# Four edits to the order of work in a four-layer trunk kernel: summing DMA, first squares, attention order, last weights

## The chip, the cores and the metric

The kernel runs on one core of one Trainium2 chip. The metric is the device time of one execution in microseconds (us). Each time is one run; the runs of the kernel before are shown below.

## The reference

The reference is a trunk of four residual layers on 512 tokens of width 1024, in float32, and a last RMS norm. The layers are pooling, short convolution, latent attention, pooling. Each normalises x, widens it with one input projection, forms a branch of width 2048 and a gate of the same width, and adds the output projection of branch times silu(gate):

```python
def pool_mixer(xn, w_in, w_grp, scale, w_out):
    u, z = split(xn @ w_in, 2)
    # per group g of 512 channels: trailing mean over 2/4/8/16 tokens, minus the token
    mixed = einsum('bsgc,gcd->bsgd', pooled, w_grp) * scale
    return (mixed * silu(z)) @ w_out

def conv_mixer(xn, w_in, conv_w, w_out):
    b, c, h, z = split(xn @ w_in, 4)
    return (b * causal_depthwise_conv(c * h, conv_w) * silu(z)) @ w_out

def mla_mixer(xn, cos, sin, w_in, q_norm, w_q_up, kv_norm, w_kv_up, w_out):
    q_lat, kv_lat, k_rope, z = split(xn @ w_in, ...)       # 384, 256, 64, 2048
    q = rms_norm(q_lat) @ w_q_up                           # 16 heads x (128 + 64 rotary)
    k_nope, v = rms_norm(kv_lat) @ w_kv_up                 # 16 heads x 128 each
    o = causal_block_attention(q_nope, rope(q_rope), k_nope, rope(k_rope), v)
    return (o * silu(z)) @ w_out
```

## The kernel before, in words

x is held transposed, as eight tiles of 128 channels by 512 tokens. Every operand of a matmul is split into a high and a low part of the reduced float32 form: ACT copies the tile into the high part, and DVE subtracts that from the tile for the low part. A product is then three matmuls (`mm3`, L258 to L260: high by high, low by high, high by low). So each block of weights needs a load, one copy on ACT and one subtraction on DVE ahead of TensorE.

The layers are written as two streams of jobs (class `Stream`). A job is a `CHUNK` (128 by 1024 weights, 24 matmuls of 512 columns) or a `PAIR`. Step j of a stream issues the loads of jobs j+1 and j+2, then runs job j, and at eight positions in it calls small steps: the splits of job j+1 and what the jobs before left over. A position over 7 falls into the next job (its number less 8). Raw weights lie in four buffers of 1024 columns ("wr") and two of 512 ("wq"), split ones in six.

A `PAIR` makes two output tiles by seven half-width products instead of eight (`seven`, L388 to L460). It needs r (1024 columns: "wr" in the profile), r4 (512: "wq") and s13 (1024: "s", in a "wr" buffer too), which is the same 512 columns loaded twice (L119, SP's queue) with r's source added to it by a summing DMA on GpSimd's queue (L120). Its splits have fixed places: ah (from r) at position 4, al and sh (from s13) at 5, sl and ch (from r4) at 6, cl and the sums into r and r4 (L399, L400) at 7, th at 10 and tl at 11 (L393 on ACT, L396 on DVE). A summing DMA waits until both halves have landed, and a load waits until the last reader of its buffer is done: r of a later pair takes the buffer of an earlier s13, whose last reader is L399; s13 takes that of an earlier r, whose last reader is tl.

Only TensorE, ACT and DVE follow the order written in a stream. GpSimd, SP and the whole attention loop are ordered by a scheduler that knows the dependences.

The pooling layers multiply u by R (the scale of the norm, L322, L580), sum it over a window on GpSimd (L617, one to four adds), subtract on DVE (L623 to L625) and split. The first layer starts on x while it loads (`first_two`, called as `pre`): it makes the high and low parts of each tile of x (L348, L349) and multiplies at once; R follows from the squares of x (L276, L282), their sum over channels on TensorE, and a broadcast (`close`, L295 to L322). "Forms" (L359 to L382) are four sums and differences of neighbouring tiles of x, which `seven` needs.

In attention, head h goes through `scores` (L1018 to L1030, softmax with it, normalised on GpSimd in L1032), `turn_p` (ten transposes, pj, L1045), and `mix` (values by turned scores, po, L1057 to L1060). `stage_a(h+1)` makes queries and keys of the next head (pq and pk, 15 matmuls) and splits them (qh, ql, kh, kl: L158, L161). For every fourth head sixteen copies of the rotary part are issued on SP (L993, "qrs").

The tail is the second pooling layer's output projection, with tokens on the partitions. `token_major` runs three quarters of it as jobs; the last quarter follows the stream, with four more loads (L1249) and eight splits of 512 columns (L158, L161, `split`).

Of the kernel before, what the change touches and what calls it, by code (L numbers as in the profile page):

```python
# [23 lines left out]
H = 16  # L24
# [40 lines left out]
def trunk_kernel(ctx: ExitStack, tc: tile.TileContext, a):  # L65
# [28 lines left out]
    def f(t):  # L94
        return t.bitcast(F32)
# [17 lines left out]
    def load_pair(src):  # L113

        r, r4, s13 = wt("wr", "wr", F32), wp.tile([P, S], F32, tag="wq", name=nm("wq"), bufs=2), wt("s13", "wr", F32)
        nc.sync.dma_start(r, src[:, :CH])
        nc.sync.dma_start(r4, src[:, CH + S :])
        for q in range(2):
            nc.sync.dma_start(s13[:, q * S : (q + 1) * S], src[:, CH : CH + S])  # L119
        nc.gpsimd.dma_start(s13, src[:, :CH], accum_op=ALU.add)  # L120
        return r, r4, s13

# [62 lines left out]
    class Stream:  # L185
# [3 lines left out]
        def __init__(self):  # L189
            self.jobs, self.at, self.later, self.raw, self.ready = [], 0, Steps(), {}, {}  # L190

# [3 lines left out]
        def load(self, j):  # L195
            if j < len(self.jobs) and j not in self.raw:
                kind, src, _ = self.jobs[j]
                self.raw[j] = kind[0](src) if kind else None

# [14 lines left out]
        def step(self):  # L214
            j = self.at
            self.at += 1
            self.load(j + 1)
            self.load(j + 2)
            now, self.later = self.later, Steps()
            now.put(self.prepare(j + 1), 2 if self.jobs[j][0] is PAIR and self.jobs[j + 1 :] and self.jobs[j + 1][0] is not PAIR else 0, first=True)  # L220
            self.jobs[j][2](self.ready.pop(j, None), now)
            now(7)
            left, self.later = self.later, Steps()
            self.later.put(now.at, -8)
            self.later.put(left.at)
# [7 lines left out]
    def load_chunk(src, width=CH):  # L233
        raw = wt("wr", "wr", F32, width)
        nc.sync.dma_start(raw, src)
        return raw

# [14 lines left out]
    def wchunk(src, width=CH, pool=False):  # L252
        w, steps = prepare_chunk(load_chunk(src, width), width, pool)
        Steps(steps)(2)
        return w
# [540 lines left out]
    def mla_layer(stream, xn, begin, cos_sin, nxt):  # L796
# [273 lines left out]
        for h in range(H):  # L1070
# [10 lines left out]
            scores(h)  # L1081
            extra(1)
            if h:
                mix(h - 1)
            extra(2)
            if h + 1 < H:
                stage_a(h + 1)
            extra(3)
# [31 lines left out]
    def first_two():  # L1120

        pre = [ps("pt") for _ in range(2)]
        for k in range(KD):
# [16 lines left out]
            for m in range(2):  # L1140
                wh, wl = w0[m, hf]
                if k == m == 0:
# [4 lines left out]
                    continue  # L1147
                mm3(pre[m], wh[:, c], wl[:, c], *xn0.xs[k], first=(k == 0), last=(k == KD - 1))

        for m in range(KD):  # L1150
            s1.later.put({m: [lambda m=m: xn0.st.add(xt[m])]})
        s1.later.put({10: [xn0.st.close]})
        for kk in range(KK):
            s1.later.put(xn0.forms(kk), 24 + 16 * kk)
        return pre

    pool_layer(s1, 0, xn0, half, at=(4, 6), pre=first_two)
    xn = nxt
# [24 lines left out]

    def token_major(stream, c, hf, ys, then):

        pos = []

        def run(wl, now, kp):
            if kp == 0:
                pos.extend(ps("po") for _ in range(NT))  # L1190
# [16 lines left out]
    tail = {}  # L1207

    def last_half(hf, ys):
        if hf == 0:  # L1210
            for c in range(2):
                token_major(s2, c, 0, ys, add_tok)
        else:
            token_major(s2, 0, 1, ys, finish)
            tail["ys"] = ys
# [29 lines left out]
    ys = tail["ys"]  # L1245
    wres = {}
    for kk in range(4):
        raw = wt("wr", "wr", F32)
        nc.sync.dma_start(raw, w[1, 4 + kk])  # L1249
        for e in range(2):  # L1250
            wres[2 * kk + e] = split(raw[:, e * S : (e + 1) * S], "w")
    for i in range(NT):
# [116 lines left out]
```

## Time and profile before

| what | us |
| --- | --- |
| median of 3 runs (lowest, highest) | 1501.44 (1498.5, 1502.46) |
| the profiled execution: its own time, its span | 1502.28, 1500.5 |
| TensorE busy in the span | 1451.2 |
| DVE, ACT, GpSimd busy | 1086.7, 686.9, 258.3 |

The profile is of one execution. Times in it count from the start of its span. A row of waits gives an engine, the line that waited, what released it, the us in total, the times and the longest. In a row of the timeline, the first number is the start and the second how long the group was busy; what stands in brackets is the idle time of the engine before it and what ended that. "PEclk" is the clock granted to TensorE as a share of full speed.

### The profile page before, as it was taken

How to read it: one execution, taken by the hardware profiler on the slowest of the kernel's cores; microseconds unless marked ns; L12 is line 12 of the kernel's file. 1: busy time of each engine (PE TensorE's matmuls, PEld its weight loads, DVE VectorE, ACT ScalarE, POOL GpSimd, SP SyncE). 2: the span in 40 equal slices, each digit the busy share in tenths (PEclk: the TensorE clock that was granted, in tenths of full speed). 3: DMA queues.
4: the chain of work that ended last, by engine and by line, in shares of the span. 5: the costliest groups of instructions: out<-in, count | busy, mean ns of one | idle time of the engine just before them, and what ended most of it. 6: DMA issues, size and time to landing. Idle time of an engine off the chain costs nothing. (4 is left out here: it accounts for less than half of the span.)

```text
span 1500.5 us, 22412 instructions
## 1 busy us (share of the span) xinstructions
PE 1451.2 (97%) x8560; PEld 1273.3 (85%) x8560; DVE 1086.7 (72%) x1771; ACT 686.9 (46%) x1174; POOL 258.3 (17%) x291
## 2 busy tenths in 40 slices
PE   9999999999999999999999999999999999999997
PEld 7788797888999889999879988788888798888886
DVE  5885556659988878998688976667755487655854
ACT  4352233445554425555355655555633355323333
POOL 2413106021001000000211001121201122311502
PEclk9999999999999999999999999999999999999999
DMA  6243354325676457666236642122122434343431
GB/s 229 70 121 105 102 137 99 127 89 120 179 185 162 139 125 191 168 181 194 86 97 169 159 148 74 55 66 84 43 84 85 113 106 115 132 108 117 113 113 57
DMA packets 65147, 181.71 MB, mean 121 GB/s; under 512 B 8080, under 2 KB 8080, under 8 KB 65040
## 3 DMA queue, kind: packets, MB, share of 16 engines
q1 hardware_dynamic: 56688, 151.44, 31.7%
q0 software_dynamic: 7488, 27.27, 10.9%
q8 instruction: 67, 1.10, 0.3%
q10 hardware_dynamic: 864, 1.57, 0.3%
q14 instruction: 40, 0.33, 0.1%
HBM read 173.70 MB, written 2.10 MB: 117 GB/s over the span
## 5 line engine op out<-in xcount | busy, mean ns | idle before, releaser
L248 DVE TENSOR_TENSOR wl<-wr,wh 128x1024 fp32r<-128x1024 f32 (+1 forms) x140 | 173.1, 1236 | 55.9 <-ACT wh L245 54.7
L245 ACT ACTIVATE wh<-wr 128x1024 fp32r<-128x1024 f32 (+1 forms) x140 | 144.4, 1034 | 147.7 <-PE o L259 47.7
L260 PE MATMUL o<-yh,wl 128*128 128x512 f32 x384 | 151.3, 394 | 1.9 <-DVE wl L248 1.9
L259 PE MATMUL o<-yl,wh 128*128 128x512 f32 x384 | 151.3, 394 | 0.2 <-DVE yl L667 0.2
L258 PE MATMUL o<-yh,wh 128*128 128x512 f32 x384 | 150.9, 393 | 0.1
L260 PE MATMUL pt<-xh,wl 128*128 128x512 f32 x367 | 145.3, 397 | 4.0 <-DVE wl L248 4.0
L258 PE MATMUL pt<-xh,wh 128*128 128x512 f32 x367 | 146.2, 398 | 2.7 <-ACT wh L245 2.5
L259 PE MATMUL pt<-xl,wh 128*128 128x512 f32 x367 | 145.2, 396 | 0.6 <-DVE xl L349 0.6
L396 DVE TENSOR_TENSOR sl<-s,sh 128x1024 fp32r<-128x1024 f32 x52 | 65.4, 1259 | 35.2 <-ACT sh L393 32.8
L440 ACT ACTIVATE kept<-bv 128x256 f32<-128x256 f32 x52 | 19.9, 383 | 152.6 <-PE bv L426 90.7
L260 PEld LDWEIGHTS o<-yh,wl 128*128 128x128 f32 x384 | 72.1, 188 | 19.2 <-DVE wl L248 2.8
L260 PEld LDWEIGHTS pt<-xh,wl 128*128 128x128 f32 x367 | 69.5, 189 | 21.6 <-DVE wl L248 5.3
L259 PEld LDWEIGHTS o<-yl,wh 128*128 128x128 f32 x384 | 72.1, 188 | 17.2 <-DVE yl L667 0.5
L258 PEld LDWEIGHTS o<-yh,wh 128*128 128x128 f32 x384 | 72.1, 188 | 17.0 <-ACT yh L664 0.5
L258 PEld LDWEIGHTS pt<-xh,wh 128*128 128x128 f32 x367 | 69.5, 189 | 19.9 <-ACT wh L245 3.8
L259 PEld LDWEIGHTS pt<-xl,wh 128*128 128x128 f32 x367 | 69.5, 189 | 16.5 <-DVE xl L349 1.0
L120 POOL DMA_DIRECT2D s<-in_conv_in x30 | 26.0, 865 | 329.6 <-DMA s<-in_conv_in 105.4
L617 POOL TENSOR_TENSOR s<-u 128x527 f32<-128x527 f32 x32 | 50.0, 1562 | 180.6 <-DVE u L580 146.5
L282 POOL TENSOR_TENSOR sq<-sq,sq 128x512 f32<-128x512 f32 x25 | 39.6, 1585 | 211.3 <-ACT sq L276 210.9
L396 DVE TENSOR_TENSOR al<-wr,ah 128x1024 fp32r<-128x1024 f32 x52 | 64.1, 1233 | 14.2 <-ACT ah L393 12.1
L617 POOL TENSOR_TENSOR s<-s 128x525 f32<-128x525 f32 (+2 forms) x48 | 69.8, 1454 | 14.4 <-PE pm L259 11.1
L393 ACT ACTIVATE sh<-s 128x1024 fp32r<-128x1024 f32 x52 | 54.9, 1055 | 35.1 <-DMA s<-in_conv_in 17.8
(308 smaller groups left out, 4575.2 us busy)
## 6 DMA issues: line engine op xcount, KB each, us to landing
wr<-in_conv_in SPq DMA_DIRECT2D x34, 512.0 KB, 5.6
wr<-in_pool_out SPq DMA_DIRECT2D x32, 512.0 KB, 3.3
wr<-in_pool_u SPq DMA_DIRECT2D x30, 512.0 KB, 3.9
s<-in_conv_in SPq DMA_DIRECT2D x60, 256.0 KB, 4.6
s<-in_conv_in POOLq DMA_DIRECT2D x30, 512.0 KB, 6.2
wr<-in_pool_z SPq DMA_DIRECT2D x18, 512.0 KB, 4.0
wr<-in_pool_grp SPq DMA_DIRECT2D x16, 512.0 KB, 3.3
wr<-in_conv_out SPq DMA_DIRECT2D x16, 512.0 KB, 3.5
```

Of the source, the lines that this page charges most:

```text
L120: nc.gpsimd.dma_start(s13, src[:, :CH], accum_op=ALU.add)
L245: nc.scalar.activation(h, raw, AF.Copy)
L248: (nc.gpsimd if pool else nc.vector).tensor_tensor(out=l, in0=raw, in1=f(h), op=ALU.subtract)
L258: nc.tensor.matmul(out, ah, bh, start=first, stop=False)
L259: nc.tensor.matmul(out, ah, bl, start=False, stop=False)
L260: nc.tensor.matmul(out, al, bh, start=False, stop=last)
L282: eng.tensor_tensor(out=self.sum, in0=self.sum, in1=sq, op=ALU.add)
L393: return lambda: nc.scalar.activation(h, t, AF.Copy)
L396: return lambda: nc.vector.tensor_tensor(out=l, in0=t, in1=f(h), op=ALU.subtract)
L440: nc.scalar.activation(dst, src, AF.Copy)
L617: nc.gpsimd.tensor_tensor(out=nx[:, lo:], in0=cur[:, lo:], in1=cur[:, lo - d : S + PAD - d], op=ALU.add)
```

## The change

1. `load_pair` issues the two halves of s13 first, then r and r4. The summing DMA is no longer issued with them: it is a small step at position 4 of the same job.
2. First layer: the squares of x stand between the tiles of `first_two` (those of tiles 0 to 5; the last two follow at position 0 of the next job). Their sum is closed at position 3 instead of 10, the rows of the statistic stand at 3 and 5 instead of 4 and 6, and the four forms stand at 48, 56, 64, 72 instead of 24, 40, 56, 72.
3. Attention: `stage_a(h + 1)` stands ahead of `mix(h - 1)`.
4. The loads and splits of the last quarter's weights become small steps of the last four jobs of the stream (`resident`): loads at positions 0 or 4, copies on ACT at 8 to 13, subtractions on DVE two positions later.

```diff
     def load_pair(src):
 
-        r, r4, s13 = wt("wr", "wr", F32), wp.tile([P, S], F32, tag="wq", name=nm("wq"), bufs=2), wt("s13", "wr", F32)
+        s13 = wt("s13", "wr", F32)
+        for q in range(2):
+            nc.sync.dma_start(s13[:, q * S : (q + 1) * S], src[:, CH : CH + S])
+        r, r4 = wt("wr", "wr", F32), wp.tile([P, S], F32, tag="wq", name=nm("wq"), bufs=2)
         nc.sync.dma_start(r, src[:, :CH])
         nc.sync.dma_start(r4, src[:, CH + S :])
-        for q in range(2):
-            nc.sync.dma_start(s13[:, q * S : (q + 1) * S], src[:, CH : CH + S])
-        nc.gpsimd.dma_start(s13, src[:, :CH], accum_op=ALU.add)
-        return r, r4, s13
+        return (r, r4, s13), {4: [lambda: nc.gpsimd.dma_start(s13, src[:, :CH], accum_op=ALU.add)]}
...
             now, self.later = self.later, Steps()
+            now.put(self.loads.at)
+            self.loads = Steps()
...
             scores(h)
             extra(1)
+            if h + 1 < H:
+                stage_a(h + 1)
+            extra(2)
             if h:
                 mix(h - 1)
-            extra(2)
-            if h + 1 < H:
-                stage_a(h + 1)
             extra(3)
...
-        for m in range(KD):
-            s1.later.put({m: [lambda m=m: xn0.st.add(xt[m])]})
-        s1.later.put({10: [xn0.st.close]})
+            if k >= 2:
+                xn0.st.add(xt[k - 2])
+
+        for m in range(KD - 2, KD):
+            s1.later.put({0: [lambda m=m: xn0.st.add(xt[m])]})
+        s1.later.put({3: [xn0.st.close]})
         for kk in range(KK):
-            s1.later.put(xn0.forms(kk), 24 + 16 * kk)
+            s1.later.put(xn0.forms(kk), 48 + 8 * kk)
         return pre
 
-    pool_layer(s1, 0, xn0, half, at=(4, 6), pre=first_two)
+    pool_layer(s1, 0, xn0, half, at=(3, 5), pre=first_two)
...
+    def resident(now, kp):
+
+        for kk, n, at in ((0, 0, 8), (1, 0, 12), (2, 1, 12), (3, 2, 10)):
+            if n == kp:
+                raw = wt("wr", "wr", F32)
+                wres.update({2 * kk + e: (ut("wh", F32R), ut("wl", F32R)) for e in range(2)})
+                now.put({4 if kp else 0: [lambda raw=raw, kk=kk: nc.sync.dma_start(raw, w[1, 4 + kk])]})
+                for e in range(2):
+                    (h, l), half = wres[2 * kk + e], raw[:, e * S : (e + 1) * S]
+                    now.put({at + e: [lambda h=h, half=half: nc.scalar.activation(h, half, AF.Copy)],
+                             at + 2 + e: [lambda h=h, l=l, half=half: nc.vector.tensor_tensor(out=l, in0=half, in1=f(h), op=ALU.subtract)]})
...
-            token_major(s2, 0, 1, ys, finish)
+            token_major(s2, 0, 1, ys, finish, resident)
...
-    wres = {}
-    for kk in range(4):
-        raw = wt("wr", "wr", F32)
-        nc.sync.dma_start(raw, w[1, 4 + kk])
-        for e in range(2):
-            wres[2 * kk + e] = split(raw[:, e * S : (e + 1) * S], "w")
```

SP's queue in the convolution layer, two pairs, before: L116 is r (wr), L119 the two halves of s13 (s), L117 is r4 (wq).

```order
L116 DMA wr_3497<-in_conv_in 128x1024
L119 DMA s_668_3499<-in_conv_in 128x512 x2
L117 DMA wq_3498<-in_conv_in 128x512
L116 DMA wr_3630<-in_conv_in 128x1024
L119 DMA s_687_3632<-in_conv_in 128x512 x2
L117 DMA wq_3631<-in_conv_in 128x512
```

The same place now (L117 the halves, L119 r, L120 r4):

```order
L117 DMA s_666_3497<-in_conv_in 128x512 x2
L119 DMA wr_3500<-in_conv_in 128x1024
L120 DMA wq_3501<-in_conv_in 128x512
L117 DMA s_685_3630<-in_conv_in 128x512 x2
L119 DMA wr_3633<-in_conv_in 128x1024
L120 DMA wq_3634<-in_conv_in 128x512
```

The halves of s13 have changed places with r. They wait for what r waited for (L399 of an earlier pair), and r waits for what they waited for (tl).

TensorE in a head of the attention loop, before: the end of the key product (pk) and the first transposes (pj); the twelve matmuls of the value mix (po) stand ahead of pq and pk there.

```order
L258 MATMUL pk_10851<-lnh_8439,wh_10360 128x512
L259 MATMUL pk_10851<-lnl_8440,wh_10360 128x512
L260 MATMUL pk_10851<-lnh_8439,wl_10361 128x512
L1045 MATMUL pj_10875<-con,p_10773 128x128
L1045 MATMUL pj_10875<-con,p_10774 128x128
```

The same place now, from the end of pk into the value mix; the other four of po and the transposes follow.

```order
L261 MATMUL pk_10837<-lnh_8439,wh_10346 128x512
L262 MATMUL pk_10837<-lnl_8440,wh_10346 128x512
L263 MATMUL pk_10837<-lnh_8439,wl_10347 128x512
L1060 MATMUL po_10848<-th_10695,vh_10133 128x512
L1061 MATMUL po_10848<-tl_10696,vh_10133 128x512
L1062 MATMUL po_10848<-th_10695,vl_10134 128x512
L1060 MATMUL po_10848<-th_10697,vh_10144 128x384
L1061 MATMUL po_10848<-tl_10698,vh_10144 128x384
L1062 MATMUL po_10848<-th_10697,vl_10145 128x384
L1060 MATMUL po_10848<-th_10699,vh_10155 128x256
L1061 MATMUL po_10848<-th_10699,vh_10155 128x256
```

The value mix has moved in between the key product and the transposes, after which the next scores read the split keys.

ACT at the end of the program, before: the last copies of the stream's chunks (wh, L245), the four squares of the finished rows (fsq), and then the copies of the last quarter's weights (wh, L158).

```order
L245 ACTIVATE wh_14657<-wr_14618 128x1024
L245 ACTIVATE wh_14685<-wr_14655 128x1024
L1224 ACTIVATE fsq_14729,ssq<-xtok_12513 128x512
L1224 ACTIVATE fsq_14736,ssq<-xtok_12649 128x512
L1224 ACTIVATE fsq_14743,ssq<-xtok_13075 128x512
L1224 ACTIVATE fsq_14750,ssq<-xtok_13198 128x512
L158 ACTIVATE wh_14756<-wr_14754 128x512
L158 ACTIVATE wh_14760<-wr_14754 128x512
```

The same place now: L1227 is the copy of the last quarter's weights, L248 that of the stream's chunks, L1245 the squares.

```order
L248 ACTIVATE wh_14669<-wr_14618 128x1024
L1227 ACTIVATE wh_14625<-wr_14622 128x512
L1227 ACTIVATE wh_14628<-wr_14627 128x512
L1227 ACTIVATE wh_14630<-wr_14627 128x512
L248 ACTIVATE wh_14711<-wr_14667 128x1024
L1227 ACTIVATE wh_14672<-wr_14671 128x512
L1227 ACTIVATE wh_14674<-wr_14671 128x512
L1227 ACTIVATE wh_14714<-wr_14713 128x512
L1227 ACTIVATE wh_14716<-wr_14713 128x512
L1245 ACTIVATE fsq_14768,ssq<-xtok_12513 128x512
```

All eight copies have moved from behind the squares to between the chunks' copies. On SP their four loads stand among those of the last chunks.

More of the change, by code (lines that the diff above doesn't have):

```diff
@@ L189, in __init__ @@
         def __init__(self):
-            self.jobs, self.at, self.later, self.raw, self.ready = [], 0, Steps(), {}, {}
+            self.jobs, self.at, self.later, self.loads, self.raw, self.ready = [], 0, Steps(), Steps(), {}, {}
         def add(self, kind, src, run):
@@ L197, in load @@
                 kind, src, _ = self.jobs[j]
-                self.raw[j] = kind[0](src) if kind else None
+                self.raw[j], steps = kind[0](src) if kind else (None, {})
+                self.loads.put(steps)
         def prepare(self, j):
@@ L235, in load_chunk @@
         nc.sync.dma_start(raw, src)
-        return raw
+        return raw, {}
     def prepare_chunk(raw, width=CH, pool=False):
@@ L252, in wchunk @@
     def wchunk(src, width=CH, pool=False):
-        w, steps = prepare_chunk(load_chunk(src, width), width, pool)
+        w, steps = prepare_chunk(load_chunk(src, width)[0], width, pool)
         Steps(steps)(2)
@@ L1182, in trunk_kernel, with token_major @@
     w = a["pool_out1"]
-    def token_major(stream, c, hf, ys, then):
+    def token_major(stream, c, hf, ys, then, stay=None):
         pos = []
         def run(wl, now, kp):
+            if stay:
+                stay(now, kp)
             if kp == 0:
@@ L1207, in trunk_kernel @@
     tail = {}
+    wres = {}
+    def resident(now, kp):
[8 more added lines that the diff above has]
+                             at + 2 + e: [lambda h=h, l=l, half=half: nc.vector.tensor_tensor(out=l, in0=half, in1=f(h), op=ALU.subtract)]})
     def last_half(hf, ys):
```

## The prediction

> **What bounds the kernel now.** I read the busy times on the page first, then the waits of TensorE over the whole run, then the same waits stretch by stretch, and last the timelines of the engines behind each wait. The page's first section and one of its groups:
>
> ```profile
> PE 1451.2 (97%) x8560; PEld 1273.3 (85%) x8560; DVE 1086.7 (72%) x1771; ACT 686.9 (46%) x1174; POOL 258.3 (17%) x291
> L260 PE MATMUL pt<-xh,wl 128*128 128x512 f32 x367 | 145.3, 397 | 4.0 <-DVE wl L248 4.0
> ```
>
> TensorE is busy for 1451.2 us of a span of 1500.5, so it idles for 49.3 us in all. The change removes no matmul. It can win only these waits and what they cause. Two costs come on top of the idle time, and the stretches show them (PE, PEld, DVE, ACT and POOL busy, then the granted clock, the DMA share and GB/s):
>
> ```profile
> 40.00:50.00 10.00, 10.00 (x44) 8.07 (x43) 5.73 (x8) 3.86 (x6) 3.50 (x5) 1.00 0.20 77
> 50.00:60.00 10.00, 10.00 (x45) 8.07 (x44) 9.90 (x14) 2.85 (x4) 5.15 (x6) 1.00 0.16 54
> 70.00:75.00 5.00, 5.00 (x15) 3.97 (x14) 4.86 (x12) 1.89 (x3) 0.00 (x0) 0.59 0.28 99
> 254.00:259.00 5.00, 4.51 (x25) 4.51 (x26) 4.96 (x6) 0.74 (x3) 3.49 (x2) 0.66 0.00 2
> 378.00:505.00 127.00, 123.12 (x1020) 120.89 (x1019) 111.50 (x159) 68.42 (x114) 10.21 (x17) 1.00 0.67 175
> 1469.00:1474.00 5.00, 4.32 (x13) 3.27 (x14) 4.63 (x6) 4.03 (x8) 3.29 (x3) 0.66 0.00 2
> ```
>
> First, 44 wide matmuls in 10 us start 0.227 us apart, although one lasts 0.397: each overlaps its forerunner by 0.17, and a wait loses that overlap. I count 0.17 us per wait. Second, after some waits the clock drops: at 0.66 over 5 us, 34% of 5 = 1.7 us of work are lost, at 0.59 some 2.05 us.
>
> **The change part by part.** *Summing DMA (conv, and the gates of the attention layer).* TensorE's waits in the three stretches (us in total, times, longest), in this order 378 to 505, 560 to 700, and of 765 to 886 the one that matters:
>
> ```profile
> PE bv L420 <- ACT sh L393: 1.8, 2, 1.0
> PE bv L426 <- DVE sl L396: 1.5, 2, 0.8
> PE bx L426 <- DVE tl L396: 0.5, 3, 0.2
> ...
> PE bx L426 <- DVE tl L396: 1.4, 2, 0.9
> PE bv L426 <- DVE sl L396: 0.7, 1, 0.7
> ...
> PE bx L426 <- DVE tl L396: 1.2, 2, 1.0
> ```
>
> They end on the splits of the sum tile or on tl, two steps behind it on DVE. What those splits wait for, in 378 to 505, then one pair step there, and last the median landing of such loads and of the summing DMAs:
>
> ```profile
> DVE sl L396 <- ACT sh L393: 13.5, 10, 3.7
> ...
> ACT sh L393 <- DMA s<-in_conv_in: 9.7, 4, 3.8
> ...
> 411.11 0.86 POOL L120 DMA_DIRECT2D s<-in_conv_in  x1 [9.93 <-DVE cl L396]
> ...
> 411.47 0.33 SPq L116 DMA_DIRECT2D wr<-in_conv_in  x1
> 414.70 1.08 SPq L119 DMA_DIRECT2D s<-in_conv_in  x2
> ...
> 420.22 1.06 ACT L393 ACTIVATE sh<-s 128x1024 fp32r<-128x1024 f32 x1 [3.50 <-DMA s<-in_conv_in]
> ...
> 427.43 1.04 ACT L393 ACTIVATE ah<-wr 128x1024 fp32r<-128x1024 f32 x1
> ...
> s<-in_conv_in POOLq DMA_DIRECT2D x11, 512.0 KB, 5.8
> wr<-in_conv_in SPq DMA_DIRECT2D x10, 512.0 KB, 5.7
> ```
>
> DVE idles 127 - 111.5 = 15.5 us there, 13.5 of them because ACT's sh waits for the summing DMA; so DVE has room, once the sum is there. In the changed order the two halves are issued where r was: 414.70 - 411.47 = 3.2 us earlier. The summing DMA waits for their landing, so it starts 3.2 us earlier too (the one that sh awaits at 420.22 was issued at 411.11, a step after its halves). That nearly covers the longest waits of sh, 3.5 and 3.8. The waits above sum to 7.1 us in 12 waits, + 12 x 0.17 = 9.1 us, and I take all of it: 9. Bounds: 12 if short waits under the list's threshold go as well, 4 if half the lateness comes back. The price lies on r, which now is issued 3.2 us later: it landed at 411.47 + 5.7 = 417.2 and is split at 427.43, ten us on, so 7 are left and it costs nothing. Behind the waiting r on SP's queue stands only the 256 KB load of its own pair; wq keeps its place.
>
> The Trainium skill, "SBUF — State Buffer", section "SBUF: two separate sides", speaks against this: a DMA from the GpSimd queue has its descriptors written by GpSimd, which VectorE can lock out. By that the summing DMA would land as late as VectorE lets it, and the term would shrink to the rival "lands as late" below; no row here shows it.
>
> *Same edit in the pool layers.* One stall there, just ahead of the stretch 254 to 259 above, and the row on VectorE behind it:
>
> ```profile
> PE bx L426 <- DVE al L396: 3.3, 1, 3.3
> ...
> 250.64 0.17 DVE L623 TENSOR_TENSOR hd<-s,con 128x16 f32<-128x16 f32 x1 [4.48 <-POOL s L617]
> ```
>
> GpSimd's last window sum stood behind a summing DMA that waited for its halves; VectorE waited 4.48 us for it, and al stood behind. With its lost clock (1.7) and overlap this stall is 3.3 + 0.17 + 1.7 = 5.2 us. The summing DMA now stands ahead of all four sums of that tile, with halves issued several us earlier, so the last sum ends earlier, but the sums start later. I take 2, with bounds 0 and 5.2.
>
> *Attention order.* The waits of 950 to 1092 and, of 925 to 946, the last; then the first and last of the sixteen rotary copies and VectorE's wait for them:
>
> ```profile
> PE s L1019 <- DVE kl L161: 3.3, 4, 1.3
> PE s L1018 <- ACT kh L158: 0.3, 1, 0.3
> ...
> PE pj L1045 <- POOL p L1032: 2.4, 1, 2.4
> ...
> 928.84 0.51 SPq L993 DMA_DIRECT2D qrs<-qah  x1
> ...
> 939.53 0.59 SPq L993 DMA_DIRECT2D qrs<-qbl  x1
> ...
> 939.78 0.69 DVE L1026 CUSTOM_DVE_ANT_0 p<-s,con 128x512 f32<-128x512 f32 x1 [5.94 <-DMA qrs<-qah]
> ```
>
> The scores of a head wait for the splits of its own k. Before, only ten transposes lay between pk and those scores; now the value mix's twelve matmuls lie there too, six of them 384 or 512 wide. At 0.227 us or less each that is some 2 us, more than the longest wait, 1.3. All five waits go: 3.6 + 5 x 0.17 = 4.4, I take 4. The other stall stays: softmax's output reuses buffers that the rotary copies read, and these come one by one over 939.53 - 928.84 = 10.7 us. If the k split ahead of it is no longer late, TensorE only waits longer there. One more weight load now stands ahead of the sixteen, at about the 0.6 us per issue that they show. Bounds: 1, if that load and the weights of the next q and k (needed 2 us earlier) take 3 back, and 7, if the stall on p goes too (2.4 and its overlap).
>
> *Start.* TensorE's waits from 12 to 100; the table of scales on ACT; the squares; and the first form on VectorE:
>
> ```profile
> PE pt L260 <- DVE wl L248: 3.2, 2, 2.4
> PE pt L258 <- ACT wh L245: 1.6, 2, 1.3
> PE pm L260 <- DVE wl L248: 0.7, 1, 0.7
> ...
> 42.31 0.60 ACT L322 ACTIVATE R<-pr 128x512 f32<-128x512 f32 x1 [1.98 <-PE pr L320]
> ...
> L276 ACT ACTIVATE sq<-x 128x512 f32<-128x512 f32 x8 | 4.4, 615 | 0.0
> ...
> 37.88 0.47 DVE L363 SCALAR_TENSOR_TENSOR d<-x,par,g 128x256 f32<-128x256 f32 x1
> ...
> 39.58 1.47 DVE L382 TENSOR_TENSOR fl<-d,fh 128x512 fp32r<-128x512 f32 x2
> ```
>
> The waits are 5.5 us in five places, 6.4 with overlap, and the low clock about 3.4 more (2.05 in 70 to 75 and the rest before it): 9.8. VectorE is full from 50 on (9.90 of 10) and half idle before (5.73), since nothing of the first tiles can go on before R at 42.31. The squares now run while x loads, their sum closes seven positions earlier, and R comes with its place on TensorE, one job of 24 matmuls (5.5 us) less the delay below. Against that, the first form (37.88 to 41.05, 3.2 us) leaves VectorE's idle time for its full time, and four forms follow each other. And six squares stand ahead of the last x split on ACT: 6 x 0.5 = 3 us, part of it in waits for x, so I count 1.2 on TensorE. So VectorE gains 5.5 - 1.2 = 4.3 and pays 3.2; 1.1 net, plus the window means that are done before 50, some 3 more, less the 1.2: I take 3. Bounds: -3 (the stretch stays full and the delays add) and 9.8.
>
> *Tail.* The last wait of the run, and ACT ahead of it:
>
> ```profile
> PE po L258 <- ACT wh L158: 2.1, 1, 2.1
> ...
> 1466.05 0.64 ACT L1224 ACTIVATE fsq<-xtok 128x512 f32<-128x512 f32 x1 [14.50 <-DVE xtok L1222]
> ```
>
> The last weights' splits stood behind four squares on ACT, which had idled 14.5 us before. Now they run in that idle time, their loads two jobs earlier. 2.1 + 0.17 and the clock's 1.7: 4.0; I take 3.5, bounds 2 and 4.
>
> *Clock.* The 2.1 us wait of the tail is followed by 0.66 (1469 to 1474). The Trainium skill, "TensorE: Matmul & The Clock Gate", section "Why this matters for your kernels", asks only that idle gaps stay under some 3 us; by it this wait would have cost no clock. The row decides; by the page the tail would give 2.3.
>
> Sum: 9 + 2 + 4 + 3 + 3.5 = 21.5 us. The profiled execution's own time is 1502.28, 0.84 above the median 1501.44 of the runs; 1501.44 - 21.5 = 1479.9, so 1480.
>
> **The rivals.** *Lands as late* (0.13): the sum tile is as late as before, because the DMA share is 0.67 and an earlier issue only queues longer. For: the sum that sh got at 420.22 was issued at 411.11, 9.1 us before, with r and the next halves issued beside it. Against: the median is 5.8, so such a landing is the exception. It leaves 2 of the 9: 1487.
>
> *The start is cured* (0.15): R early enough empties VectorE's queue and no wait is long enough to lower the clock, 9.8 instead of 3, and the stall at 254 goes for 5.2 instead of 2: 10 us more, 1470. For: both stalls hang on one late instruction each. Against: VectorE at 9.90 of 10 has the same work as before.
>
> *r becomes the late load* (0.04), the one that ends slower: if r needs longer than the 7 us left to it, every pair step waits. Each us past that point costs one us in each pair step; 10 such loads in 127 us make 31 in the three stretches' 388 us, so 1 us late is 31 - 21.5 = 9.5 slower: 1511. For it speaks only that more loads now meet; the median of 5.7 speaks against.
>
> *Moved, not won* (0.03): the waits come back elsewhere, VectorE having 111.5 of 127 us busy anyway: within 4 us of before, 1500.
>
> **How the numbers follow.** The forecast has 0.65. Its terms at their low ends sum to 4 + 0 + 1 - 3 + 2 = 4, at their high ends to 38; not all ends meet, so I take 8 to 34, which gives 1467 to 1493; both likelier rivals lie inside. About 0.3% (4.5 us) is what a measurement of this kernel tells from no change. Only the two last rivals, and the low end of the sum, miss faster: faster 0.92, same 0.04, slower 0.04.
>
> **What would show it.** Right: in 378 to 505 VectorE's wait for sh falls from 13.5 to under 5, and TensorE's on sh, sl and tl to under 1; from 950 to 1092 no wait on kl or kh; R before 40; no wait on L158's wh at the end and clock 1.00 there; the wait for p near 944 still there. Wrong: ah of the pair steps waits for a DMA; the wl waits from 60 to 95 remain over 5 us; scores wait for k with weights late before them.

## The result and the profile after

| what | us |
| --- | --- |
| before: median of the runs timed beside it (lowest, highest) | 1501.95 (1498.5, 1505.5) |
| after: median of 4 runs (lowest, highest) | 1489.04 (1488.14, 1490.13) |
| ratio, 95% interval | 0.9914 [0.9896, 0.9932] |
| the profiled execution after: its own time, its span | 1488.14, 1486.4 |

The change saves 12.9 us, where 21.5 were forecast; the time lies inside the range of 1467 to 1493, near its slow end. One of the five runs of the kernel with the attention edit undone (below), the profiled one, took 2006.64 us at a granted clock of 0.655, so its trace is not used; without it that kernel's median of 1491.79 would be 1491.61. The page's first section comes first. From L240 to L1080 a line's number is three higher than before (the sum's split is L399 now, the weight splits are L248 and L251).

```profile
PE 1442.5 (97%) x8560; PEld 1271.0 (86%) x8560; DVE 1090.3 (73%) x1771; ACT 685.1 (46%) x1174; POOL 254.7 (17%) x291
```

The span is 14.1 us shorter, but TensorE's idle time fell only from 49.3 to 1486.4 - 1442.5 = 43.9, by 5.4; the other 8.7 are busy time. The same 8560 matmuls take less of it, because a wait also costs the overlap of its neighbours and sometimes the clock. The clock is the smaller part: the mean granted clock went from 0.991 to 0.992 only, which is some 2 us. Counting idle time alone would find less than half of the gain.

The stretches, as in the prediction (PE, PEld, DVE, ACT and POOL busy, then the granted clock, the DMA share and GB/s), shifted by what the program has gained there:

```profile
40.00:50.00 10.00, 10.00 (x45) 8.15 (x44) 7.67 (x9) 3.04 (x4) 6.49 (x8) 1.00 0.31 106
70.00:75.00 5.00, 2.80 (x6) 1.79 (x7) 4.47 (x9) 2.71 (x5) 0.00 (x0) 0.52 0.07 21
370.00:497.00 127.00, 126.51 (x1074) 126.30 (x1073) 119.27 (x169) 71.23 (x122) 10.21 (x17) 1.00 0.74 180
1455.00:1460.00 5.00, 5.00 (x23) 4.10 (x22) 3.52 (x9) 2.71 (x8) 3.04 (x3) 1.00 0.00 0
```

In the convolutions TensorE starts 1074 matmuls in 127 us instead of 1020, and at the tail the clock stays at 1.00. At 70 to 75 us it is worse: 6 matmuls instead of 15, at a clock of 0.52. TensorE's waits after, from 12 to 100, 370 to 500, 915 to 940 and 940 to 1085 (line, releaser, us in total, times, longest):

```profile
PE pt L261 <- ACT wh L248: 4.3, 1, 4.3
PE pt L263 <- DVE wl L251: 2.8, 3, 1.4
...
PE bx L429 <- DVE tl L399: 0.5, 1, 0.5
...
PE s L1021 <- ACT kh L158: 3.3, 1, 3.3
PE pj L1048 <- POOL p L1035: 2.2, 1, 2.2
...
PE s L1022 <- DVE kl L161: 2.2, 3, 1.0
```

The start has one wait of 4.3 us and three shorter ones, 7.1 us in these two rows, where before it had five of at most 2.4 us, 5.5 in all. The convolutions have almost none left. In attention the wait for p stands as it did, three waits for kl are left, and the longest wait for kh has grown from 2.0 us to 3.3.

Where the time went is best read from the clock times of the same matmul in both traces. A row that groups a tile's matmuls ends with the start of the first and the last of them. Here are the marks of before, in the program's order (output projections o, the first of the attention layer's projections pa, the last value mix of attention, the last layer's broadcast pr, its last z projection pt, its last group product pm, and the run's last po):

```profile
L259 PE MATMUL o<-yl,wh x384: 387/393/507, 150.0 to 1175.1; 128*128 128x512 f32 x192
L259 PE MATMUL pa<-lnl,wh x24: 388/393/397, 877.1 to 1013.6; 128*128 128x512 f32 x24
L1058 PE MATMUL po<-tl,vh x48: 273/337/397, 908.5 to 1099.5; 128*128 128x512 f32 x16, 128*128 128x384 f32 x16, 128*128 128x128 f32 x16
L319 PE MATMUL pr<-dg,ones x6: 392/396/502, 41.6 to 1194.3; 128*128 128x512 f32 x6
L259 PE MATMUL pt<-xl,wh x367: 387/393/628, 7.4 to 1404.0; 128*128 128x512 f32 x184
L259 PE MATMUL pm<-pll,wh x128: 387/394/402, 84.0 to 1444.5; 128*128 128x512 f32 x128
L259 PE MATMUL po<-wl,yh x136: 276/393/796, 1311.5 to 1493.6; 128*128 128x512 f32 x120, 128*128 128x256 f32 x16
```

And the same marks after:

```profile
L262 PE MATMUL o<-yl,wh x384: 387/393/497, 151.6 to 1164.4; 128*128 128x512 f32 x192
L262 PE MATMUL pa<-lnl,wh x24: 390/396/398, 868.7 to 1005.3; 128*128 128x512 f32 x24
L1061 PE MATMUL po<-tl,vh x48: 271/338/397, 903.5 to 1088.7; 128*128 128x512 f32 x16, 128*128 128x384 f32 x16, 128*128 128x128 f32 x16
L322 PE MATMUL pr<-dg,ones x6: 388/391/505, 37.8 to 1182.1; 128*128 128x512 f32 x6
L262 PE MATMUL pt<-xl,wh x367: 387/393/628, 7.4 to 1391.5; 128*128 128x512 f32 x184
L262 PE MATMUL pm<-pll,wh x128: 387/394/402, 87.3 to 1434.6; 128*128 128x512 f32 x128
L262 PE MATMUL po<-wl,yh x136: 275/392/404, 1299.1 to 1479.4; 128*128 128x512 f32 x120, 128*128 128x256 f32 x16
```

One mark more from the timelines of ACT, R of the second layer, before and after:

```profile
351.66 0.58 ACT L322 ACTIVATE R<-pr 128x512 f32<-128x512 f32 x1
```

```profile
354.14 0.58 ACT L325 ACTIVATE R<-pr 128x512 f32<-128x512 f32 x1
```

After less before at each mark gives how far the program is behind (+) or ahead (-), and the steps between marks give what each stage lost or won:

| stage, up to | at the mark | step | forecast |
| --- | --- | --- | --- |
| first layer's start, first o (150.0, 151.6) | +1.6 | +1.6 | -3 |
| rest of the first pool layer, R (351.66, 354.14) | +2.5 | +0.9 | with the last layer: -2 |
| convolution and gates, first pa (877.1, 868.7) | -8.4 | -10.9 | -9 |
| attention, last mix (1099.5, 1088.7) | -10.8 | -2.4 | -4 |
| the norm of the last layer, pr (1194.3, 1182.1) | -12.2 | -1.4 | none |
| the last layer to its last pt (1404.0, 1391.5) | -12.5 | -0.3 | none |
| its pairs, last pm (1444.5, 1434.6) | -9.9 | +2.6 | in the -2 |
| the tail, last po (1493.6, 1479.4) | -14.2 | -4.3 | -3.5 |

Three terms are about as forecast (convolution, attention, tail), two have the wrong sign (the start and the pooling layers).

### The profile page after: what moved, and what is told of

The parts are those of the page before. It is cut to its first block, busy times and chain, and to the rows that moved or that the text cites. A ratio compares the mean times of both kernels' runs of the same rounds, so it can differ in the third digit from the quotient of the medians.

```text
span 1486.4 us, 22441 instructions
## 1 busy us (share of the span) xinstructions
PE 1442.5 (97%) x8560; PEld 1271.0 (86%) x8560; DVE 1090.3 (73%) x1771; ACT 685.1 (46%) x1174; POOL 254.7 (17%) x291
## 5 line engine op out<-in xcount | busy, mean ns | idle before, releaser
L251 DVE TENSOR_TENSOR wl<-wr,wh 128x1024 fp32r<-128x1024 f32 (+1 forms) x140 | 173.3, 1238 | 52.5 <-ACT wh L248 52.0
L248 ACT ACTIVATE wh<-wr 128x1024 fp32r<-128x1024 f32 (+1 forms) x140 | 144.4, 1034 | 139.6 <-PE o L262 47.7
L399 DVE TENSOR_TENSOR sl<-s,sh 128x1024 fp32r<-128x1024 f32 x52 | 64.6, 1242 | 22.1 <-ACT sh L396 22.1
L399 DVE TENSOR_TENSOR al<-wr,ah 128x1024 fp32r<-128x1024 f32 x52 | 64.2, 1234 | 15.4 <-ACT ah L396 13.4
L620 POOL TENSOR_TENSOR s<-s 128x525 f32<-128x525 f32 (+2 forms) x48 | 66.1, 1377 | 14.5 <-PE pm L262 11.2
L443 ACT ACTIVATE kept<-bx 128x512 f32<-128x512 f32 x104 | 50.9, 490 | 37.1 <-PE bx L429 37.1
```

The costliest lines, as they stand in the source:

```text
L248: nc.scalar.activation(h, raw, AF.Copy)
L251: (nc.gpsimd if pool else nc.vector).tensor_tensor(out=l, in0=raw, in1=f(h), op=ALU.subtract)
L399: return lambda: nc.vector.tensor_tensor(out=l, in0=t, in1=f(h), op=ALU.subtract)
L443: nc.scalar.activation(dst, src, AF.Copy)
L620: nc.gpsimd.tensor_tensor(out=nx[:, lo:], in0=cur[:, lo:], in1=cur[:, lo - d : S + PAD - d], op=ALU.add)
```

## The experiments

Each kernel is the changed one with the edit shown, timed in five rounds against the kernel before. Differences are between the medians and 1489.04. The kernel before took 1501.61 to 1503.74 us beside them, 1501.95 beside the changed kernel, and by the ratios the differences come out up to 1 us larger or smaller. One ratio's interval is some 0.2% wide to either side, 3 us, so a difference of 2 or 3 us shows nothing by itself; it is read together with the marks, which a table at the end of this section gives for all traces.

**One edit undone at a time.** The start (the squares, their closing, the rows of the statistic and the forms are where they were):

```diff
-        s1.later.put({3: [xn0.st.close]})
+        s1.later.put({10: [xn0.st.close]})
...
-            s1.later.put(xn0.forms(kk), 48 + 8 * kk)
+            s1.later.put(xn0.forms(kk), 24 + 16 * kk)
```

> The changed kernel with the first layer's edit undone (squares, close and forms where they were before); the other three parts stay. Theory A, from the waits of the two traces: the stretch from 12 to 100 us lost 10.3 us to waits and low clock before and 11.8 after, so the start edit costs 1.5 us and this kernel is about 1.5 us faster than the changed one: 1487.5. Rival B, the prediction's term: the edit wins 3 us, and this kernel is 3 us slower: 1492.

Measured 1489.96 us, ratio 0.9917 [0.9894, 0.9939]: 0.9 us above the changed kernel, between the two. The start edit as a whole is worth nothing that can be measured. In the trace the first o stands at 151.7, no earlier than the changed kernel's 151.6, but that is a loss ahead of the edit: the granted clock was 0.79 from 6 to 12 us, where it is 1.00 in the two other traces. From pr, at 43.3, to the first o this kernel takes 108.4 us, just as the kernel before.

The load order of the pairs:

```diff
+        for q in range(2):
+            nc.sync.dma_start(s13[:, q * S : (q + 1) * S], src[:, CH : CH + S])
+        nc.gpsimd.dma_start(s13, src[:, :CH], accum_op=ALU.add)
+        return (r, r4, s13), {}
```

> The changed kernel with the old load order (r, r4, the halves, and the summing DMA at once); the rest stays. Theory A, from the traces: conv and the attention layer's gates gained 8.7 us, the pool layers lost about 0.6, so about 8 us slower than the changed kernel: 1497, with the wait of VectorE for sh in conv back at some 13 us. Rival B: most of that gain comes from elsewhere (the shifted start of the layers), and this kernel loses under 4 us: below 1493.

Measured 1497.43 us, ratio 0.9976 [0.9957, 0.9995]: 8.4 us of the gain go. It is the largest part, and theory A's size. In its profile ACT's sh waits for the summing DMA again, which it does nowhere in the changed kernel from 370 to 500. VectorE's wait for sh is back too, but at 8.2 us in 8 times, not at the 13 that were expected. First ACT's wait with the edit undone, then VectorE's in the changed kernel:

```profile
ACT sh L396 <- DMA s<-in_conv_in: 4.3, 4, 1.7
```

```profile
DVE sl L399 <- ACT sh L396: 5.2, 6, 0.9
```

The attention order:

```diff
-            if h + 1 < H:
-                stage_a(h + 1)
-            extra(2)
             if h:
                 mix(h - 1)
+            extra(2)
+            if h + 1 < H:
+                stage_a(h + 1)
```

> The changed kernel with the value mix ahead of the next head's queries and keys again; the rest stays. Theory A, from the traces: 4.0 us slower, 1493, with waits of the scores on kl and kh from 940 to 1085 of about 3.6 us instead of 2.2, and one wait near 930 and one near 944 instead of two larger ones near 923 and 936. Rival B: the stall on the rotary copies swallows all of it and the time stays within 1 us of 1489.

Measured 1491.79 us, ratio 0.9931 [0.9906, 0.9956]: 2.75 us slower, nearer to the first theory, and about the marks' 2.4. The waits that theory A named are not known for this kernel.

The tail:

```diff
-            token_major(s2, 0, 1, ys, finish, resident)
+            token_major(s2, 0, 1, ys, finish)
...
+    for kk in range(4):
+        raw = wt("wr", "wr", F32)
+        nc.sync.dma_start(raw, w[1, 4 + kk])
+        for e in range(2):
+            wres[2 * kk + e] = split(raw[:, e * S : (e + 1) * S], "w")
```

> The changed kernel with the last quarter's weights loaded and split behind the stream again; the rest stays. Theory A, from the traces: the tail lost 4.25 us before and 0.01 after, so 4.2 us slower: 1493.2, with the wait of po on wh (2.1 us) back and a clock of 0.66 after it. Rival B: without the lowered clock, 2.5 us slower: 1491.5.

Measured 1494.49 us, ratio 0.9944 [0.9924, 0.9964]: 5.4 us. The wait is back, and with it a low clock, 0.75 in the stretch from 1457 to 1462 and, one microsecond later, 0.66 from 1458 to 1463, as theory A had it (the waits from 1440 to 1480, then the first stretch):

```profile
PE po L261 <- ACT wh L158: 2.1, 1, 2.1
```

```profile
1457.00:1462.00 5.00, 2.94 (x9) 2.12 (x9) 4.06 (x8) 5.00 (x13) 5.00 (x4) 0.75 0.00 0
```

The four parts sum to 0.9 + 8.4 + 2.75 + 5.4 = 17.5 us against 12.9 for the whole; with 3 us of uncertainty on each, that is no contradiction.

**Where the forms stand in the first layer.** The early squares stay; only the forms move, first to where VectorE had idle time, then back to their old places.

```diff
-            s1.later.put(xn0.forms(kk), 48 + 8 * kk)
+            s1.later.put(xn0.forms(kk), 8 + 8 * kk)
```

> The changed kernel with the four forms of the first layer at positions 8, 16, 24 and 32 instead of 48 to 72: into the time before the table of scales (R, 38.5 us), when VectorE idles. Theory A: the stretch from 40 to 95 us is bounded by VectorE, and the forms (about 3.2 us each, up to 5 where GpSimd adds beside them) are what overfills it, so most of its 11.8 us of lost time goes: 8 us faster than the changed kernel, 1481, with the wait of TensorE on ACT's wh (4.3 us) gone. Rival B: VectorE waits for GpSimd's window sums there, whatever else it has to do, and the time stays within 2 us of 1489.

Measured 1490.1 us, ratio 0.9915 [0.9893, 0.9936]: no gain, the rival's time. The wait for wh is gone, but waits for wl have taken its place (12 to 100 us). The rival's reason is not borne out: VectorE has no wait from 45 to 72 us and is busy for 9.83 of 10 us both from 50 to 60 and from 60 to 70. And not every form has left the crowded stretch: one of the four still runs there, two of its operations at 1.28 us.

```profile
PE pt L263 <- DVE wl L251: 5.3, 4, 2.4
```

```diff
-            s1.later.put(xn0.forms(kk), 48 + 8 * kk)
+            s1.later.put(xn0.forms(kk), 24 + 16 * kk)
```

> The changed kernel with the forms at 24, 40, 56 and 72 again, and the early squares kept. Theory A (the forms overfill VectorE after R): only the first form moves back ahead of R, 3.2 us of VectorE, so 2 to 3 us faster: 1486. Rival B (where the forms stand doesn't matter): 1489.

Measured 1491.55 us, ratio 0.9927 [0.9906, 0.9947]: 2.5 us slower, so neither theory. With the early R, forms in the old places are worse than with the late one: the first o starts at 155.2 us, 3.6 behind the changed kernel. Next, the forms behind the window means of the second group:

```diff
-            s1.later.put(xn0.forms(kk), 48 + 8 * kk)
+            s1.later.put(xn0.forms(kk), 64 + 8 * kk)
```

> The loop of the first layer that puts the three first forms at 48 + 8 kk puts them at 64 + 8 kk: behind the bunches of window means of the second group instead of among them; the early squares and all else are as in the changed kernel. Theory: the start loses its time since the split wh at L248 stands behind a bunch (the wait of 4.3 us of the tensor engine at 72 us); with the forms behind it, that wait is gone and the time is 1484.5 to 1486. Rival: GpSimd's sums and the order in which the groups close bind, and the wait only moves to later jobs: 1488 to 1490, with waits of the tensor engine of 7 us or more on wh, wl between 12 and 100 us as now.

Measured 1486.44 us, ratio 0.9891 [0.9874, 0.9908]: 2.6 us faster, just outside the window that was given, on the theory's side. The first o starts at 148.1 us, 3.5 ahead of the changed kernel, and from 60 to 95 us the forms' operations take 0.48 us each. The two largest waits of the start (12 to 100 us; two more follow, of 1.2 and 0.5 us), then the stretch from 70 to 80 with the clock at 1.00, and last the same stretch of the changed kernel, at 0.66:

```profile
PE pt L263 <- DVE wl L251: 2.3, 3, 1.4
PE pt L261 <- ACT wh L248: 1.4, 1, 1.4
```

```profile
70.00:80.00 10.00, 9.95 (x42) 7.83 (x43) 9.57 (x19) 6.29 (x10) 1.05 (x1) 1.00 0.49 120
```

```profile
70.00:80.00 10.00, 7.80 (x23) 5.78 (x24) 9.30 (x20) 6.38 (x10) 1.05 (x1) 0.66 0.20 53
```

**Whose time the forms take.** The forms between 62 and 66 us last 1.28 us, with one of GpSimd's additions beside each. So the additions of the first two groups went to VectorE:

```diff
-                    nc.gpsimd.tensor_tensor(out=nx[:, lo:], in0=cur[:, lo:], in1=cur[:, lo - d : S + PAD - d], op=ALU.add)
+                    (nc.vector if pre is not None and g < 2 else nc.gpsimd).tensor_tensor(out=nx[:, lo:], in0=cur[:, lo:], in1=cur[:, lo - d : S + PAD - d], op=ALU.add)
```

> The window sums of the first two groups of the first layer (12 additions at L620) run on the vector engine instead of GpSimd; all else as in the changed kernel. Theory: the two engines hold each other up there, so that operations of the vector engine last as long as GpSimd's additions beside them (1.28 us where the same form takes 0.47 alone); with the additions on the vector engine the forms of L366 to L368 are at 0.5 us each again, and the time is 1485 to 1487. Rival: 12 additions more fill the vector engine (9.8 of 10 us busy between 50 and 70 us already), the splits wl come later: 1489 to 1494.

Measured 1489.44 us, ratio 0.9913 [0.9896, 0.9931]: no gain, and both theories have a point. The mechanism is there: between 30 and 80 us the mean of a form's operation (L367) falls from 880 to 479 ns, and that of the small sums L628 from 454 to 176. But the additions cost VectorE what they give back (8 of 708 ns and 4 of 706 make 8.5 us; from 12 to 100 us it is busy for 71.79 us, before this edit 71.74). The changed kernel, then this one:

```profile
L628 DVE TENSOR_TENSOR s<-hd,u 128x16 f32<-128x16 f32 x8 | 3.6, 454 | 0.3
...
L367 DVE SCALAR_TENSOR_TENSOR d<-x,par,g 128x256 f32<-128x256 f32 x2 | 1.8, 880 | 0.0
```

```profile
L628 DVE TENSOR_TENSOR s<-hd,u 128x16 f32<-128x16 f32 x8 | 1.4, 176 | 0.3
...
L367 DVE SCALAR_TENSOR_TENSOR d<-x,par,g 128x256 f32<-128x256 f32 x2 | 1.0, 479 | 0.0
```

**The rotary copies.** Every second one on GpSimd's queue:

```diff
-                    nc.sync.dma_start(f(st)[32 * q : 32 * q + 32, :], f(src)[32 * hh : 32 * hh + 32, :])
+                    (nc.gpsimd if q % 2 else nc.sync).dma_start(f(st)[32 * q : 32 * q + 32, :], f(src)[32 * hh : 32 * hh + 32, :])
```

> The changed kernel with every second rotary copy (8 of each 16) issued on GpSimd's queue instead of SP's. Theory A: the wait of the transposes on p near 936 us (2.2 us, and the lowered clock behind it) is the chain of sixteen issues on SP, 10.7 us long; halved it ends 4 us earlier and the wait goes: 3.5 us faster, 1485.5. Rival B: GpSimd needs 0.87 us for an issue and normalises p behind them, or the transfers themselves are what lasts, and the wait stays: 1489.

Measured 1483.78 us, ratio 0.9874 [0.9849, 0.9898]: 5.3 us faster, and the marks put 5.1 of it between the first pa and the last mix. Near 930 us VectorE's softmax waited 5.87 us for these copies and started at 931.92; now it waits 1.38 and starts at 928.91. TensorE's wait for p is gone, its wait of 3.3 us for kh is not, and of the 2.2 us for kl 0.8 are left (886 to 1092 us). The clock has no part in it: it is 0.89 from 915 to 945 in both traces.

```profile
PE s L1022 <- DVE kl L161: 0.8, 2, 0.6
```

**The pool layers alone.** Old order of the loads there, the new one in the convolutions and gates; the summing DMA is issued with the loads everywhere.

```diff
+        pool = src.tensor.name.find("pool") >= 0
...
-        return (r, r4, s13), {4: [lambda: nc.gpsimd.dma_start(s13, src[:, :CH], accum_op=ALU.add)]}
+        if pool:
+            copies()
+        nc.gpsimd.dma_start(s13, src[:, :CH], accum_op=ALU.add)
+        return (r, r4, s13), {}
```

> The changed kernel with the old load order in the two pooling layers alone; conv and the attention layer keep the halves first. The summing DMA is issued with the loads again in all layers, which leaves GpSimd's order in conv as it was. Theory A: in the pooling layers GpSimd's window sums stand behind a summing DMA that waits for its halves, which costs about 3 us around 1400 and nothing around 255, where the old order stalls as well: 1486. Rival B: 1489, the losses there have another cause.

Measured 1486.4 us, ratio 0.9893 [0.9868, 0.9919]: 2.6 us faster, with the convolutions as fast as in the changed kernel (514.6 us from R to the first pa in both). So the new order costs time in the pool layers, and where the step that issues the summing DMA stands in the program makes no difference to the convolutions: what counts there is that the halves are loaded first. The last layer's stretch of the changed kernel, then of this one:

```profile
1400.00:1420.00 20.00, 15.84 (x115) 15.04 (x115) 18.91 (x26) 10.50 (x19) 5.71 (x6) 0.91 0.26 79
```

```profile
1400.00:1420.00 20.00, 18.07 (x151) 17.81 (x151) 19.34 (x26) 11.65 (x21) 5.09 (x4) 1.00 0.30 97
```

**Together.** First the last two edits, then these and the forms at 64.

> Both edits that gained alone, together: half of the rotary copies are issued on the GpSimd queue, and the pool layers load in the old order, with the summing DMA among the loads; the pairs of the convolutions and gates, the start, the attention order and the tail as in the changed kernel. Theory: the two places have nothing in common, so the gains add: 1489.0 - 5.3 - 2.6 = 1481 (1480 to 1482.5). Rival: the summing DMA and the rotary copies share the GpSimd queue, or the next stage takes back what is won: 1483.5 or more, no better than the rotary copies alone.

Measured 1481.83 us, ratio 0.986 [0.9842, 0.9878].

> The three edits that gained, together: half of the rotary copies on the GpSimd queue, the old load order in the pool layers, the first forms at 64 + 8 kk. Theory: start, attention and last pool layer have nothing in common, so the gains add once more: the two edits before gave 1481.8, the forms 2.6 less, 1479 (1478 to 1480.5); the tensor engine waits at most 4 us on the splits wh, wl between 12 and 100 us, with the clock at 1.00 there. Rival: what the start wins comes back later (the wait at 225 us moves or grows): 1481 or more.

Measured 1479.91 us (1478.37 to 1480.2), ratio 0.9847 [0.983, 0.9865]: 9.1 us better than the changed kernel and 21.8 better than the 1501.69 of before beside it. The three single gains sum to 10.5, so they add within 1.4 us. The marks place them: 3.6 us at the start, 5.1 in attention and 2.6 in the last pairs, less 1.9 at the last norm, where the old load order's wait is back. This is the fastest kernel here.

**The same steps in all traces.** How long a step between two marks takes, in us, with the number of traces that the range is of. The kernel before counts as old in every row; the trace of the kernel with the attention edit undone is left out.

| step | old order or place | new |
| --- | --- | --- |
| first pr to first o | 108.4 (2), pr at 41.6 and 43.3 | 113.7 to 113.8 (6), pr at 37.6 to 39.1 |
| first o to R of the second layer | 201.6 to 203.6 (5) | 202.3 to 204.2 (8) |
| that R to first pa | 525.4 and 527.4 (2) | 513.9 to 516.0 (11) |
| first pa to last mix | 222.4 (1) | 218.7 to 220.7 (9); half of the copies moved: 214.9 (3) |
| last mix to pr of the last layer | 94.5 to 95.3 (5) | 93.2 to 93.6 (8) |
| last pt to last pm | 38.9 to 40.5 (5) | 43.1 to 44.7 (8) |
| last pm to last po | 48.8 and 49.1 (2) | 44.7 to 44.9 (11) |

The gains of the convolutions, the tail and the last norm and the loss in the last pairs repeat in every trace. In the second row the two ranges overlap, so its 0.9 us are not shown to come from the load order.

## Why the prediction was right or wrong, step by step

**Convolution and gates: right.** The forecast was 9; the marks give 10.9, and undoing the edit costs 8.4, from which its loss in the pool layers (2.1 by the marks) is already taken off. Of the two signs that were named, TensorE's waits came (0.5 us left) and VectorE's wait for sh nearly (5.2 us left where "under 5" was said). That short waits under the threshold of the list go as well was the reason for the upper bound of 12, and the marks lie between. "Lands as late" fell: VectorE is busy for 119.27 of 127 us, and still ACT's list of waits there holds none for the summing DMA any more. The DMA did not get faster (a median of 6.5 us to its landing, 5.8 before); it starts earlier. The Trainium skill ("SBUF — State Buffer", section "SBUF: two separate sides") ties the lock on the writing of descriptors to VectorE operations in a 2-port mode, and says that a two-input `tensor_tensor` has no such mode. 157 of VectorE's 169 operations in that stretch are of that kind, so the prediction's use of the rule hardly fitted them, and these runs do not test it.

**Pool layers: wrong.** The step that failed is "halves issued several us earlier, so the last sum ends earlier". The summing DMA does stand ahead of all four sums, as the prediction said, but it waits for its halves, and on GpSimd the sums stand behind that wait (the changed kernel, in order of time):

```profile
242.09 0.80 SPq L117 DMA_DIRECT2D s<-in_pool_z  x2
...
244.45 0.68 DVE L583 TENSOR_TENSOR u<-pt,R 128x512 f32<-128x512 f32 x1
...
247.38 0.87 POOL L121 DMA_DIRECT2D s<-in_pool_z  x1 [8.21 <-DMA s<-in_pool_z]
...
247.99 1.36 POOL L620 TENSOR_TENSOR s<-u 128x527 f32<-128x527 f32 x1
...
253.03 0.18 DVE L626 TENSOR_TENSOR hd<-s,con 128x16 f32<-128x16 f32 x1 [4.85 <-POOL u L613]
```

u is there at 244.45 + 0.68 = 245.13, and the sums begin at 247.99: 2.9 us lost, after which VectorE waits 4.85 us (4.48 before) and al is late again, by 3.7 (3.3 before). In a convolution GpSimd has nothing to do meanwhile (10.21 us busy in 127), so the same order is free there. In the last layer the order costs 2.6, and GpSimd stands still there as well, at a summing DMA that has come in between the window sums of one group (4.09 us, though the view names a matmul as what ended it), after which VectorE waits 3.76 us; with the old order the same operation on VectorE waits for nothing:

```profile
1386.39 0.87 POOL L121 DMA_DIRECT2D s<-in_pool_z  x1 [4.09 <-PE pt L262]
...
1389.75 0.18 DVE L626 TENSOR_TENSOR hd<-s,con 128x16 f32<-128x16 f32 x1 [3.76 <-POOL u L613]
```

The new order also gives 1.4 that the prediction had not seen: before, the last norm's sr stood behind a summing DMA in the same way, 12.44 us idle, and TensorE waited for what follows it. Before, then after:

```profile
1191.10 0.87 POOL L120 DMA_DIRECT2D s<-in_pool_z  x1 [12.44 <-DMA s<-in_pool_z]
1191.66 1.37 POOL L300 TENSOR_TENSOR sr<-sv,mhalf 128x4 f32<-128x4 f32 x1
```

```profile
1179.77 1.04 POOL L303 TENSOR_TENSOR sr<-sv,mhalf 128x4 f32<-128x4 f32 x1 [6.29 <-DVE sv L298]
```

With the old order back in the pool layers alone that wait of TensorE is back, 1.5 us as before. So the term is a loss of 0.9 + 2.6 - 1.4 = 2.1 us where a gain of 2 was taken, below the lower bound of 0, and the old order gives 2.6 back. What is shown of it is the 2.6, nearer 4 in the mean of all traces, and the 1.4; the 0.9 is not.

**Attention: right, too large.** 4 forecast, 2.4 by the marks, 2.75 by the run. The term that was too large is "All five waits go": from 940 to 1085 three waits for kl of 2.2 us in all remain of 3.6 in five. And the longest wait for kh, ahead of the sixteen copies, grew from 2.0 us to 3.3; why is open. The stall on p was rightly kept in the forecast, and the run with half of the copies on another queue shows its cause: the copies, one by one on SP's queue. That run also takes the waits for kl to 0.8. The 2.2 us of p and the 1.4 of kl make, with 0.17 of overlap each, 4 of its 5.3 us; the rest is not told apart.

**Start: wrong.** By the marks it lost 1.6 us where 3 were to be won. R did come 3.8 us earlier (pr at 37.8, not 41.6), but from there to the first o the kernel took 113.8 us, not 108.4. VectorE did fill the stretch from 40 to 50 (7.67 busy, 5.73 before). The step that failed is the balance, "VectorE gains 5.5 - 1.2 = 4.3 and pays 3.2". A form in the new place does not take its 0.47 us:

```profile
62.38 1.28 DVE L366 SCALAR_TENSOR_TENSOR d<-x,par,g 128x256 f32<-128x256 f32 x1
...
63.51 1.07 POOL L620 TENSOR_TENSOR s<-u 128x527 f32<-128x527 f32 x1
63.58 1.28 DVE L367 SCALAR_TENSOR_TENSOR d<-x,par,g 128x256 f32<-128x256 f32 x1
64.66 1.12 POOL L620 TENSOR_TENSOR s<-s 128x525 f32<-128x525 f32 x1
64.79 1.28 DVE L368 SCALAR_TENSOR_TENSOR d<-x,npar,d 128x256 f32<-128x256 f32 x1
66.10 0.48 DVE L369 SCALAR_TENSOR_TENSOR d<-x,npar,d 128x256 f32<-128x256 f32 x1
```

L366 ends at 63.66, 0.29 us after an addition that ran from 61.45 to 63.37; L367 ends at 64.86, 0.28 us after the addition that began before it (63.51 + 1.07 = 64.58), and L368 at 66.07, 0.29 after the next one (64.66 + 1.12 = 65.78); L369 stands with no addition beside it and takes 0.48. The three slow ones add 3 x 0.8 = 2.4 us. The Trainium skill, "SBUF — State Buffer", section "SBUF: two separate sides", has the rule: the port pair that VectorE and GpSimd share is locked for a whole instruction, and a VectorE operation with two inputs from SBUF waits for a GpSimd one that reads SBUF. The trace agrees (all three end 0.28 or 0.29 us behind GpSimd's), and so does the experiment with the additions on VectorE (880 to 479 ns). The forms then hold the window means behind them, these hold ACT's plh, and the weights' split wh, which starts at 71.06, is behind that on ACT: 4.3 us for TensorE, and the clock.

```profile
70.53 0.63 ACT L631 ACTIVATE plh<-s 128x512 fp32r<-128x512 f32 x1 [1.59 <-DVE s L628]
```

The forms at 64 end this, forms at 8 only move it to wl, forms in the old places make it 2.5 worse. That the edit as a whole wins nothing is shown; how much of the loss of 1.6 is the forms' own length and how much their order among the window means was not told apart. The rival that the start is cured had the right place but not the size: with the forms at 64 the clock stays at 1.00 from 12 to 100 us, but the first o (148.1) stands only 1.9 us ahead of the kernel before, where the rival had 9.8.

**Tail: right.** 3.5 forecast, 4.3 by the marks, 5.4 by the run; no wait there now.

**The clock: right.** With the tail undone, a wait of 2.1 us again comes with a low clock (0.66 over 5 us). The Trainium skill, "TensorE: Matmul & The Clock Gate", section "Why this matters for your kernels", asks only for gaps under some 3 us; the rows go on deciding against it, and the tail won the 4.3 us that hold the clock's share, not 2.3.

The other rivals fell: r is not late, and the waits did not come back in the convolutions. In sum the miss of 7.3 against the profiled 14.2 is 4.1 in the pool layers, 4.6 at the start and 1.6 in attention, less 1.9, 0.8 and 0.3 that the convolutions, the tail and the rest of the last layer gave on top. With two of five terms of the wrong sign, the time lies inside the range because the range was wide, 26 us.

## What to carry to other kernels

An order of loads that is right for one stage can be wrong for the next: ask, for each stage, what stands behind a waiting DMA issue on the engine that issues it, and change the order only where that engine is idle. Work that is moved into a busy stretch is not priced by its duration in a quiet one: look what the neighbour engine does at that moment. And a chain of waits is best cleared by looking at what the scarce queue carries: half of the rotary copies on another queue were worth twice the reordering around them.

## What the runs showed of the hardware

A VectorE operation on 128x256 elements with two inputs in SBUF lasted 1.28 us beside GpSimd's additions and 0.48 without; small ones of 128x16 took 454 ns in the mean beside them and 176 without. A wait of 2.1 us of TensorE came with a granted clock of 0.66 over 5 us, one of 4.3 with 0.52. GpSimd stood idle at the issue of a DMA that waited for another transfer, 8.21 and 12.44 us in the two rows shown, and in the first its window sums began only behind it, 2.9 us after their input was there.
